# The entry of a SwiGLU FFN in a hybrid decoder layer: weights prepared in three steps, two products taken early, matmul operands moved by 32 bytes

## The chip, the cores and the metric

The kernel runs on one core of one Trainium2 chip. The metric is the device time of one execution in microseconds (us); the time of a kernel is the median of its runs.

## What is computed

One decoder layer on x of 512 tokens by 1024 channels, float32: an RMSNorm and an input projection, an RWKV-7 group and a sparse-attention group side by side, an output projection that is added to x, and then the part that this change concerns, a dense SwiGLU with its own norm, added again, and a last norm:

```python
def swiglu(x, w_gate, w_up, w_down):
    return (jax.nn.silu(x @ w_gate) * (x @ w_up)) @ w_down
...
        h = h + jnp.concatenate([y_r, y_n], axis=-1) @ w_out[l]
        h = h + swiglu(rms_norm(h, norm_ffn[l]), w_gate[l], w_up[l], w_down[l])
    return rms_norm(h, norm_final)
```

The FFN is 2816 wide, so the gate and up products are 512 x 1024 x 5632 together.

## The kernel before, in words

**Precision.** A float32 product is made of three matmuls (`mm3`, L162 to L165): each operand is split into a rounded part `hi` (a copy on ACT, L144) and the rest `lo` (a subtraction on DVE, L146), and hi x hi, hi x lo and lo x hi are accumulated. So each operand costs one ACT and one DVE instruction (`split`, L140) before PE can use it, and each of its matmuls loads its own 128 x 128 weights.

**Gate and up.** Columns of w_gate and w_up are taken in 11 quarters of 256 columns (q = 0 to 10). A quarter multiplies a 2 x 2 block matrix (two halves of the tokens by two halves of the channels, A11, A12, A21, A22) with a 2 x 2 block of weights (gate and up by two halves of the channels, B11, B21, B12, B22) in seven products instead of eight. On the side of A these need sums S1 to S4 of the blocks, on the side of the weights T1 to T4. The order on PE is B11 x A11, B21 x A12, T2 x S2, T1 x S1, T3 x S3, B22 x S4, T4 x A22. A product (`prod`, L1168) is 24 matmuls of 256 columns; a quarter is 168, the FFN's 11 quarters 1848. The weights are the stationary operand, A the moving one. The products are collected by DVE and ACT (L1189 to L1212).

**Weights of a quarter** (`weight_side`, L1112): SP issues loads of 512 KB for B11, B21, the gate half of T1, B22 and the up half of T3; POOL issues two DMAs that add w_up onto T1 (L1141) and T3 (L1142); DVE forms T2 = T1 + B22 (L1145) and T4 = T2 + B21 (L1150); each of the seven is split. Splits go in turn to the two buffers of tag whi and the two of wlo; of quarter 0 B11 and B21 go to tag b8. The raw data lie in wraw, and T1 to T3 in t4 for even quarters and in one slot of L for odd ones.

**The norm ahead of it** (`ffn_norm`, L1070). The output projection (`accumulate`, L1011) finishes the token tiles t = 0 to 3 one after the other; after each, DVE adds the residual (L1163), ACT squares and sums (L176, L177), DVE scales (L1076, xn), PE transposes (L1086), ACT copies out of PSUM (L1088). Tiles 0 and 1 are split into A11 and A12 at once. Tiles 2 and 3 first form S3, S1, S2, S4 with tiles 0 and 1 on DVE (L1099 to L1104) and split five operands each. Quarter 0's weights are prepared in the projection, ahead of its last four blocks (`ahead`, L1156).

**What sets the order.** Each engine runs its instructions in the order that a scheduler gave them when the program was built, in which `tc.high_priority()` brings work forward and an edge of `tc.issue_after(x)` keeps a block's instructions on the engine of x behind x. DMAs are issued by SP and POOL in order too, and an issue waits until the slot that it fills is free.

**Where the tiles lie.** The tiles of all tags lie in one SBUF range in a fixed layout. In every partition the slots of L, t4, wraw, whi and wlo begin 160 bytes past a multiple of 256, those of b8 and gin 32 bytes, that of kB 64, ident 128. The parts that a matmul reads begin whole multiples of 256 bytes into their slot. S2 lies in gin, S1 in kB, S4 in b8, A11, A12, S3 and A22 in L.

**Other users of the split weights.** `parts` (L148) serves the projections. For 512-column products (L163 to L165 with 128x512) the weights are stationary and the normed x in L moves, or in the output and down projections the other way round. In the first token projection (L301), the two compressions (`job_cmp1`, L666) and the four late token jobs (`job_vt`, `job_ks`, two `job_qs`, L602 to L647) the split weights are the moving operand of 256-column matmuls: 96 + 64 + 384 of them.

Of the kernel before, what the change touches and what calls it, by code (L numbers as in the profile page):

```python
# [46 lines left out]
def hybrid_layer(ctx: ExitStack, tc: tile.TileContext, x, positions, norm_mix, w_in, mu_shift, w0, w2, a0, a2,  # L47
# [12 lines left out]

    SB_BUFS = {"L": 4, "b8": 6, "t4": 4, "t2": 3, "wraw": 3, "whi": 2, "wlo": 2}
# [104 lines left out]

    def rstd_of(src, cut=()):
# [9 lines left out]
        ACT.activation(ss[:, 1:2], ss[:, 0:1], AF.Sqrt, scale=1.0 / D, bias=bias)  # L177
# [119 lines left out]
    for t in range(NT):  # L297
        next(norm)
        if t == 0:
            w0p = parts(raw0)  # L300
# [706 lines left out]
    gain2 = st([128, D], "t4")  # L1007
    nc.sync.dma_start(gain2, bcast_row(norm_ffn))
# [41 lines left out]


# [9 lines left out]
    def operand(tag):  # L1061
        v = st([128, 2, HK, 256], tag, dtype=F32R)
# [7 lines left out]
    def ffn_norm(src):  # L1070
        xn2 = st([128, 2, D], "b8")
        for t in range(NT):
            s = src(t)
            r = rstd_of(s)
            xn = xn2[:, t % 2]
            DVE.scalar_tensor_tensor(xn, s, r, gain2, op0=OP.mult, op1=OP.mult)  # L1076
# [3 lines left out]
            def put(name, v):  # L1080
                split(v, A[name][0][:, :, c], A[name][1][:, :, c])

            for kh in range(2):
                p = ps("s")
                for i in range(HK):
                    PE.transpose(p[:, i * 128:(i + 1) * 128], xn[:, (kh * HK + i) * 128:(kh * HK + i + 1) * 128], ident)  # L1086
# [4 lines left out]
            if t >= 2:  # L1091
# [268 lines left out]
```

## Time and profile before

| | us |
|---|---|
| median of 3 runs | 758.5 |
| lowest and highest | 755.49, 758.87 |
| the profiled execution | 762.32 |
| its span, first to last instruction | 760.6 |
| granted TensorE clock, mean over the span | 0.981 |

In the profile, PE is TensorE's matmuls, PEld its weight loads, DVE is VectorE, ACT ScalarE, POOL GpSimd, SP the engine that issues most DMAs. A matmul's row has its start and duration; matmuls overlap, so the rate is read from start to start. Names stand as out<-in by tag: `ps_ra<-gin,whi` is a matmul into a PSUM bank of tag ra that moves gin over weights in whi. The tag names b8 and t4, t2 appear as b and t. L146 and the like are lines of the kernel before.

### The profile page before, as it was taken

The page shows a single profiled execution, that of the slowest core. Times are in us where ns is not written, and L with a number is a line of the kernel's source. Part 1 is how long each engine was busy: PE and PEld are TensorE (multiplying, and loading weights), DVE is VectorE, ACT ScalarE, POOL GpSimd, SP SyncE. Part 2 cuts the span into 40 slices and gives each one's busy share as a digit, 9 for nine tenths or more (in the row PEclk, how much of TensorE's full clock was granted, in tenths as well). Part 3 has the DMA queues.
Part 4 walks back from the last instruction along what each step waited for, and adds up shares of the span by engine and source line. Part 5 has one row for each costly group of instructions (what it writes and reads, how often), then busy time and mean ns, then how long its engine had stood idle before and what let it go on. Part 6 is the DMA issues. An engine that isn't in the chain of part 4 may idle for free.

```text
span 760.6 us, 14951 instructions
## 1 busy us (share of the span) xinstructions
PE 726.2 (95%) x6045; PEld 636.6 (84%) x6045; DVE 593.1 (78%) x1089; ACT 399.1 (52%) x666; POOL 164.6 (22%) x262
## 2 busy tenths in 40 slices
PE   6999999998879999999998699999999999999996
PEld 6967878898867888767787699999999999877885
DVE  5488688879868888786459496969688789999835
ACT  6398735324366866756437534535344454465424
POOL 3210053048435542454001101111102001010000
PEclk7999999999999999999998999999999999999999
DMA  7723533100061000230415747695967629443302
GB/s 249 198 85 110 166 111 110 57 2 2 3 222 30 2 2 2 58 112 1 139 56 139 165 130 177 155 229 145 225 161 194 143 81 272 172 110 111 139 0 110
DMA packets 73467, 87.02 MB, mean 114 GB/s; under 512 B 4996, under 2 KB 62934, under 8 KB 73398
## 3 DMA queue, kind: packets, MB, share of 16 engines
q1 hardware_dynamic: 60694, 72.43, 29.2%
q0 software_dynamic: 12704, 13.63, 11.6%
q8 instruction: 47, 0.77, 0.4%
q14 instruction: 22, 0.18, 0.1%
HBM read 83.96 MB, written 2.10 MB: 113 GB/s over the span
## 4 chain that ended last, share of the span: by engine, by line
PE 67%; DVE 22%; DMA 4%; issue 3%; ACT 3%; POOL 0%; SPq 0%; DVEq 0%; ACTq 0%
PE ps_ra L164 6%; PE ps_ra L165 6%; PE ps_ra L163 6%; PE ps_pj L165 6%; PE ps_pj L163 6%; PE ps_pj L164 6%; PE ps_o L1001 3%; PE ps_s L165 3%; PE ps_s L163 3%; PE ps_s L164 3%; DVE wlo L146 3%; DVE L L146 3%; PE ps_pj L993 3%; DMA L<-in_w_up_dram 2%; DVE whi L146 2%
## 5 line engine op out<-in xcount | busy, mean ns | idle before, releaser
L144 ACT ACTIVATE whi<-wraw 128x1024 fp32r<-128x1024 f32 (+1 forms) x63 | 62.5, 1030 | 36.0 <-issue 9.1
L146 DVE TENSOR_TENSOR wlo<-wraw,whi 128x1024 fp32r<-128x1024 f32 (+1 forms) x46 | 58.9, 1306 | 16.3 <-ACT whi L144 12.8
L165 PE MATMUL ps_ra<-L,wlo 128*128 128x512 f32 (+2 forms) x144 | 50.9, 355 | 0.0
L990 POOL TENSOR_SCALAR whi<-whi,m,gates 128x128 f32<-128x128 f32 (+3 forms) x64 | 42.5, 680 | 37.1 <-DVE m L988 28.8
L164 PE MATMUL ps_ra<-L,whi 128*128 128x512 f32 (+2 forms) x136 | 47.4, 348 | 1.1 <-DVE L L146 1.1
L163 PE MATMUL ps_ra<-L,whi 128*128 128x512 f32 (+2 forms) x136 | 47.0, 346 | 1.2 <-ACT L L144 1.2
L164 PE MATMUL ps_pj<-L,whi 128*128 128x512 f32 (+1 forms) x128 | 45.7, 357 | 0.0
L163 PE MATMUL ps_pj<-L,whi 128*128 128x512 f32 (+1 forms) x128 | 45.1, 357 | 0.0
L165 PE MATMUL ps_pj<-L,wlo 128*128 128x512 f32 (+1 forms) x120 | 41.2, 343 | 0.0
L987 ACT ACTIVATE whi<-whi,m 128x128 f32<-128x128 f32 (+3 forms) x64 | 35.4, 554 | 9.5 <-DVE m L986 8.3
L163 PE MATMUL ps_ra<-whi,L 128*128 128x256 f32 (+1 forms) x108 | 35.7, 332 | 0.2 <-ACT L L144 0.2
L164 PE MATMUL ps_ra<-wlo,L 128*128 128x256 f32 (+1 forms) x108 | 35.7, 330 | 0.2 <-DVE wlo L146 0.2
L165 PE MATMUL ps_ra<-whi,L 128*128 128x256 f32 (+1 forms) x108 | 35.1, 327 | 0.0
L986 DVE CUSTOM_DVE_ANT_0 whi<-ps_s,negb 128x128 f32<-128x128 f32 (+3 forms) x64 | 29.3, 484 | 5.9 <-PE ps_pj L993 2.5
L165 PE MATMUL ps_pj<-whi,L 128*128 128x256 f32 (+1 forms) x108 | 33.9, 315 | 0.0
L164 PE MATMUL ps_pj<-wlo,L 128*128 128x256 f32 (+1 forms) x108 | 33.8, 313 | 0.0
L163 PE MATMUL ps_pj<-whi,L 128*128 128x256 f32 (+1 forms) x108 | 33.6, 315 | 0.0
L1141 POOL DMA_DIRECT2D t<-in_w_up_dram x6 | 7.9, 1323 | 114.0 <-DVE whi L146 50.2
L165 PEld LDWEIGHTS ps_ra<-L,wlo 128*128 128x128 f32 (+1 forms) x144 | 27.2, 189 | 4.2 <-issue 0.5
L164 PEld LDWEIGHTS ps_ra<-L,whi 128*128 128x128 f32 (+1 forms) x136 | 25.6, 188 | 4.8 <-DVE L L146 1.3
L163 PEld LDWEIGHTS ps_ra<-L,whi 128*128 128x128 f32 (+1 forms) x136 | 25.7, 189 | 4.7 <-ACT L L144 1.4
L164 PEld LDWEIGHTS ps_pj<-L,whi 128*128 128x128 f32 x128 | 24.9, 195 | 3.4 <-DVE L L146 0.4
(685 smaller groups left out, 2561.2 us busy)
## 6 DMA issues: line engine op xcount, KB each, us to landing
wraw<-in_w_gate_dram SPq DMA_DIRECT2D x22, 512.0 KB
wraw<-in_w_in_dram SPq DMA_DIRECT2D x9, 1024.0 KB
wraw<-in_w_down_dram SPq DMA_DIRECT2D x9, 1024.0 KB
t<-in_w_up_dram POOLq DMA_DIRECT2D x12, 512.0 KB, 7.4
wraw<-in_w_up_dram SPq DMA_DIRECT2D x11, 512.0 KB
L<-in_w_up_dram POOLq DMA_DIRECT2D x10, 512.0 KB, 8.2
wraw<-in_w_out_dram SPq DMA_DIRECT2D x4, 1024.0 KB
wraw<-in_w_in_dram SPq DMA_DIRECT2D x6, 512.0 KB
```

The lines of the kernel that those rows point to most:

```text
L144: ACT.activation(hi, src, AF.Copy)
L146: (POOL if pool else DVE).tensor_sub(lo, src, hi.bitcast(F32))
L163: PE.matmul(o, lh, rh, start=start, stop=False)
L164: PE.matmul(o, lh, rl, start=False, stop=False)
L165: PE.matmul(o, ll, rh, start=False, stop=stop)
L986: DVE.tensor_tensor_reduce(pr[:, i], pS[:, i], negb[:, S - n:S], scale=-1.0, scalar=3e38, op0=OP.add, op1=OP.min, accum_out=m[:, i, 0:1])
L987: ACT.activation(pr[:, i], pr[:, i], AF.Exp, scale=-1.0, bias=m[:, i, 0:1], accum_out=m[:, i, 1:2])
L990: POOL.tensor_scalar(pr[:, i], pr[:, i], m[:, i, 2:3], gv[:, 1 + b0 + i, h:h + 1], op0=OP.mult, op1=OP.mult)
L993: PE.transpose(pT[:, j], prr[:, x, j * 128:j * 128 + 128], ident)
L1001: PE.matmul(po[q, 2 * g:2 * g + 2], vtok[:, j % (t + 1), b0 + j // (t + 1), g], pTs[:, par, j], start=False, stop=g == 1 and bs[-1] == 1 a ...
L1141: POOL.dma_start(t1, quarter(w_up, 0), accum_op=OP.add)
```

## The change

`weight_side` becomes a class `Weights` whose steps are called one by one: loads of B11 and B21 when it is made, `begin` (their splits), `load_rest` (the other loads and the adding DMAs), `middle` (T2, T1), `end` (T3, B22, T4). Quarter 0 does all but `end` ahead of the projection's last blocks, with B11, B21, T2 and T1 in b8. After the norm come, in program order, `begin` of quarter 1, kept behind the last tile's Sqrt and xn; `end` of quarter 0, kept behind the last split of S4; the first two products of quarter 0; the first two of quarter 1, kept on PE behind the last transpose; and the other five of quarter 0. From quarter 2 on the steps follow one another as before. The residual additions and the norm are given high priority, S1 and S3 change places in the norm, gain2 is loaded a little later. The slots of whi and wlo grow by 64 elements (256 bytes), paid for by a descriptor scratch of 2048 in place of 4096 bytes; the FFN's weights are placed 56 elements (224 bytes) into their slot, and split weights that move 8 elements (32 bytes), so that on L the moving operand begins 32 bytes behind the stationary one, modulo 256.

```diff
+    PAD = 64
-    def parts(raw, tags=("whi", "wlo"), pool=False, lo_pool=False):
+    def parts(raw, tags=("whi", "wlo"), pool=False, lo_pool=False, off=0):
         b, n = raw.shape[1:]
-        hi, lo = (st([128, 2048], tag, 2, F32R) for tag in tags)
-        v = [t[:, 0:b * n].rearrange("p (k n) -> p k n", n=n) for t in (hi, lo)]
+        hi, lo = (st([128, 2048 + PAD], tag, 2, F32R) for tag in tags)
+        v = [t[:, off:off + b * n].rearrange("p (k n) -> p k n", n=n) for t in (hi, lo)]
...
-            w0p = parts(raw0)
+            w0p = parts(raw0, off=8)
...
+    moving = [jobs[i][1] for i in (3, 5, 7, 9, 12, 13, 14, 15)]
...
-        wn = parts(raws.pop(0)) if raws else None
+        wn = parts(raws.pop(0), off=8 if jobs[n + 1][1] in moving else 0) if raws else None
...
-    def operand(tag):
-        v = st([128, 2, HK, 256], tag, dtype=F32R)
+    def operand(tag, off=0):
+        v = st([128, 2048 + (PAD if tag in ("whi", "wlo") else 0)], tag, dtype=F32R)[:, off:off + 2048]
+        v = v.rearrange("p (x k n) -> p x k n", x=2, n=256)
         return v[:, 0], v[:, 1]
...
-            r = rstd_of(s)
             xn = xn2[:, t % 2]
-            DVE.scalar_tensor_tensor(xn, s, r, gain2, op0=OP.mult, op1=OP.mult)
+            with tc.high_priority(offset=1000000 if t in () else None):
+                r = rstd_of(s)
+                last["xn"] = DVE.scalar_tensor_tensor(xn, s, r, gain2, op0=OP.mult, op1=OP.mult).ins
...
-                s3 = st([128, HK, 128], "t2")
-                DVE.tensor_sub(s3, a11, a21)
-                DVE.tensor_sub(a21, a22, a21)
-                DVE.scalar_tensor_tensor(a11, a21, -1.0, a11, op0=OP.mult, op1=OP.subtract)
+                s1 = st([128, HK, 128], "t2")
+                DVE.tensor_sub(s1, a22, a21)
+                DVE.tensor_sub(a21, a11, a21)
+                DVE.scalar_tensor_tensor(a11, s1, -1.0, a11, op0=OP.mult, op1=OP.subtract)
...
+        def put(self, name, v, tag=None):
+            if tag is None:
+                tag = ("whi", "wlo")[turn2[0] % 2]
+                turn2[0] += 1
+            o = operand(tag, 56 if tag != "b8" else 0)
+            split(v, *o)
+            setattr(self, name, o)
...
     def ahead():
-        first.append(weight_side(0, 2))
+        ws[0] = Weights(0)
+        ws[0].begin("b8")
+        ws[0].load_rest()
+        ws[0].middle("b8")
...
-        for f in range(2):
-            sl = slice(f * 512, f * 512 + 512)
-            DVE.tensor_add(x2[:, t, sl], banks[f], x2[:, t, sl])
-        next(norm)
+        with tc.high_priority():
+            for f in range(2):
+                sl = slice(f * 512, f * 512 + 512)
+                DVE.tensor_add(x2[:, t, sl], banks[f], x2[:, t, sl])
+            next(norm)
...
+    ws[1] = Weights(1)
+    with tc.issue_after(last["sq"]), tc.issue_after(last["xn"]):
+        ws[1].begin()
+    with tc.issue_after(last["S4"][0]), tc.issue_after(last["S4"][1]):
+        ws[0].end()
+    first_products(0)
+    with tc.issue_after(last["pe"]):
+        first_products(1)
+    last_products(0)
+    for q in range(1, NF // 2):
+        if q > 1:
+            ws[q] = Weights(q)
+            ws[q].begin()
+        ws[q].load_rest()
+        ws[q].middle()
+        ws[q].end()
+        if q > 1:
+            first_products(q)
+        last_products(q)
...
-    nc = _bacc.Bacc("TRN2", target_bir_lowering=False, num_devices=1, dynamic_dma_scratch_size=4096)
+    nc = _bacc.Bacc("TRN2", target_bir_lowering=False, num_devices=1, dynamic_dma_scratch_size=2048)
```

`first_products(q)` and `last_products(q)` are the old loop's body cut behind the second product; the buffers u and g0 of quarter 1 lie in t4 and smask.

## Rows read from the trace of the kernel before

**Rows 1.** The page's parts 1 and 5: busy us, share, count; busy, mean ns, idle.
```profile
PE 726.2 (95%) x6045; PEld 636.6 (84%) x6045; DVE 593.1 (78%) x1089; ACT 399.1 (52%) x666; POOL 164.6 (22%) x262
...
L144 ACT ACTIVATE whi<-wraw 128x1024 fp32r<-128x1024 f32 (+1 forms) x63 | 62.5, 1030 | 36.0 <-issue 9.1
L146 DVE TENSOR_TENSOR wlo<-wraw,whi 128x1024 fp32r<-128x1024 f32 (+1 forms) x46 | 58.9, 1306 | 16.3 <-ACT whi L144 12.8
```

**Rows 2.** By stage: us; PE, PEld, DVE, ACT, POOL busy (count); PEclk, DMA share, GB/s.
```profile
380.00:404.50 24.50, 24.50 (x115) 20.33 (x114) 15.24 (x21) 12.36 (x20) 0.00 (x0) 1.00 0.13 43
404.50:441.60 37.10, 27.98 (x193) 26.64 (x192) 27.44 (x38) 19.89 (x31) 5.21 (x4) 0.86 0.69 156
...
481.60:642.50 160.90, 160.37 (x1346) 160.16 (x1345) 133.65 (x148) 73.82 (x83) 17.95 (x14) 1.00 0.69 176
...
143.00:204.00 61.00, 57.38 (x746) 54.61 (x745) 55.12 (x130) 19.93 (x36) 31.48 (x68) 0.97 0.01 2
```

**Rows 3.** The timeline of PE at the entry: start us, duration us, [idle before <-releaser].
```profile
404.33 0.27 PE L1086 MATMUL ps_s<-ident,b 128*128 128x128 f32 x1
407.37 0.47 PE L1086 MATMUL ps_s<-ident,b 128*128 128x128 f32 x1 [2.01 <-ACT L L1088]
411.12 0.58 PE L164 MATMUL ps_pj<-L,b 128*128 128x256 f32 x1 [1.36 <-DVE L L146]
420.36 0.38 PE L163 MATMUL ps_ra<-L,whi 128*128 128x256 f32 x1 [1.23 <-ACT L L144]
437.39 0.39 PE L165 MATMUL ps_pj<-L,whi 128*128 128x256 f32 x1 [3.26 <-DVE whi L146]
441.63 0.28 PE L164 MATMUL ps_ra<-L,wlo 128*128 128x256 f32 x1
```

**Rows 4.** The timeline of PE: first matmuls of products in the third quarter.
```profile
461.56 0.28 PE L163 MATMUL ps_s<-L,whi 128*128 128x256 f32 x1
464.44 0.28 PE L163 MATMUL ps_pj<-L,wlo 128*128 128x256 f32 x1
467.32 0.28 PE L163 MATMUL ps_ra<-gin,whi 128*128 128x256 f32 x1
470.17 0.28 PE L163 MATMUL ps_s<-kB,wlo 128*128 128x256 f32 x1
472.99 0.28 PE L163 MATMUL ps_pj<-L,whi 128*128 128x256 f32 x1
...
481.58 0.28 PE L163 MATMUL ps_pj<-L,wlo 128*128 128x256 f32 x1
```

**Rows 5.** The timeline of PE: eight transposes of the last tile, merged.
```profile
416.78 1.04 PE L1086 MATMUL ps_s<-ident,b 128*128 128x128 f32 x8
```

**Rows 6.** The timeline of DVE at the entry.
```profile
404.11 1.22 DVE L146 TENSOR_TENSOR wlo<-t,wlo 128x1024 fp32r<-128x1024 f32 x1
405.25 0.68 DVE L1163 TENSOR_TENSOR L<-ps_rb,L 128x512 f32<-128x512 f32 x1
...
413.46 1.27 DVE L1076 SCALAR_TENSOR_TENSOR b<-L,ss,t 128x1024 f32<-128x1024 f32 x1
...
424.23 0.69 DVE L146 TENSOR_TENSOR b<-L,b 128x512 fp32r<-128x512 f32 x1
...
434.98 1.23 DVE L1145 TENSOR_TENSOR L<-L,wraw 128x1024 f32<-128x1024 f32 x1 [5.79 <-DMA L<-in_w_up_dram]
```

**Rows 7.** The timelines of ACT, POOL and SP (SPq issues DMAs) around the entry.
```profile
409.87 1.05 ACT L176 ACTIVATE t<-L 128x1024 bf16<-128x1024 f32 x1
...
429.18 1.29 POOL L1141 DMA_DIRECT2D L<-in_w_up_dram  x1 [11.57 <-DVE t L1196]
430.34 1.43 POOL L1142 DMA_DIRECT2D L<-in_w_up_dram  x1
...
385.65 0.37 SPq L1125 DMA_DIRECT2D wraw<-in_w_gate_dram  x1
```

**Rows 8.** The timeline of DVE in the ninth quarter.
```profile
593.89 1.22 DVE L1145 TENSOR_TENSOR L<-L,wraw 128x1024 f32<-128x1024 f32 x1 [6.05 <-DMA L<-in_w_up_dram]
```

More of the change, by code (lines that the diff above doesn't have):

```diff
@@ L1080, in put @@
             def put(name, v):
-                split(v, A[name][0][:, :, c], A[name][1][:, :, c])
+                hi, lo = (o[:, :, c] for o in A[name])
+                last[t] = last[name] = ACT.activation(hi, v, AF.Copy).ins, DVE.tensor_sub(lo, v, hi.bitcast(F32)).ins
             for kh in range(2):
@@ L1154, in hybrid_layer, with __init__, quarter, begin @@
-    first = []
+    class Weights:
+        def __init__(self, q):
+            def quarter(w, kh):
+                return w[kh * 512:kh * 512 + 512, q * 256:q * 256 + 256].rearrange("(k p) n -> p k n", p=128)
+            r = st([128, 2, HK, 256], "wraw")
+            self.b11, self.b21 = r[:, 0], r[:, 1]
+            nc.sync.dma_start(self.b11, quarter(w_gate, 0))
+            nc.sync.dma_start(self.b21, quarter(w_gate, 1))
+            self.q, self.quarter = q, quarter
+        def put(self, name, v, tag=None):
[5 more added lines that the diff above has]
+            setattr(self, name, o)
+        def begin(self, tag=None):
+            with tc.high_priority():
+                self.put("B11", self.b11, tag)
+                self.put("B21", self.b21, tag)
+        def load_rest(self):
+            self.b22 = st([128, 2048], "wraw")[:, 0:1024].rearrange("p (k n) -> p k n", n=256)
+            if self.q % 2:
+                tt = st([128, 4, HK, 256], "L")
+                self.t1, self.t2, self.t3 = (tt[:, i] for i in range(3))
+            else:
+                self.t1, self.t2, self.t3 = (st([128, HK, 256], "t4") for _ in range(3))
+            nc.sync.dma_start(self.t1, self.quarter(w_gate, 0))
+            nc.sync.dma_start(self.b22, self.quarter(w_up, 1))
+            nc.sync.dma_start(self.t3, self.quarter(w_up, 0))
+            with tc.high_priority():
+                POOL.dma_start(self.t1, self.quarter(w_up, 0), accum_op=OP.add)
+                POOL.dma_start(self.t3, self.quarter(w_up, 1), accum_op=OP.add)
+        def middle(self, tag=None):
+            with tc.high_priority():
+                DVE.tensor_add(self.t2, self.t1, self.b22)
+                self.put("T2", self.t2, tag)
+                self.put("T1", self.t1, tag)
+        def end(self):
+            with tc.high_priority():
+                self.put("T3", self.t3)
+                self.put("B22", self.b22)
+                DVE.tensor_add(self.t2, self.t2, self.b21)
+                self.put("T4", self.t2)
@@ L1176, in prod, with first_products @@
         return o
-    hid, hid4 = [], []
-    for q in range(NF // 2):
+    hid, hid4, part = [], [], {}
+    def first_products(q):
         if q % 2 == 0:
-            h4 = st([128, 4, S], "b8") if q < NF // 2 - 1 else st([128, 2, S], "t4")
-            hid4.append(h4)
-        hq = h4[:, q % 2 * 2:q % 2 * 2 + 2]
-        hid += [hq[:, j] for j in range(2)]
-        w = weight_side(q) if q else first[0]
-        u, g0, v, u1 = (st([128, 2, 256], tag) for tag in ("t2", "t2", "t2", ("lora", "smask")[q % 2]))
-        p = prod(w["B11"], A["A11"])
+            part["h"] = st([128, 4, S], "b8") if q < NF // 2 - 1 else st([128, 2, S], "t4")
+            hid4.append(part["h"])
+        hq = part["h"][:, q % 2 * 2:q % 2 * 2 + 2]
+        hid.extend(hq[:, j] for j in range(2))
+        w = ws[q]
+        u, g0 = st([128, 2, 256], "t4" if q == 1 else "t2"), st([128, 2, 256], "smask" if q == 1 else "t2")
+        p = prod(w.B11, A["A11"])
         with tc.high_priority():
             ACT.activation(u, p, AF.Copy)
-        p = prod(w["B21"], A["A12"])
+        p = prod(w.B21, A["A12"])
         with tc.high_priority():
@@ L1258, in hybrid_layer @@
         a11, a21, a12, a22 = (h[:, :, x] for h in (one, two) for x in (left, right))
-        first, last = n == 0, n == 1
+        lead, end = n == 0, n == 1
         t1, t2 = block4(a, 0, "wraw"), block4(b, 1, ("gin", "kB")[n])
-        t3 = st([128, 4, 512], "wraw") if first else None
-        t3 = [t3[:, 2 * i:2 * i + 2] if first else st([128, 2, 512], "t4") for i in range(2)]
+        t3 = st([128, 4, 512], "wraw") if lead else None
+        t3 = [t3[:, 2 * i:2 * i + 2] if lead else st([128, 2, 512], "t4") for i in range(2)]
         for i in range(2):
@@ L1266, in hybrid_layer @@
         DVE.tensor_sub(a21, a22, a21)
-        multiply(m1, a_side(a11), b_side(t1), first, last)
+        multiply(m1, a_side(a11), b_side(t1), lead, end)
         DVE.tensor_add(a11, a21, a11)
```

72 lines of the change are left out of this document (22 added, 50 removed).

## Prediction

> **What bounds the kernel now.** I read the page's engine list first: PE is busy 726.2 us of 760.6, DVE 593.1 [rows 1]. That says matmuls bound most of the time, and leaves two questions: where PE waits, and how fast it goes where it doesn't. The table by stage answers the first: the entry of the FFN, 404.5 to 441.6 us, has PE busy for 27.98 of 37.1 us at a granted clock of 0.86, where the stretch before it has no gap and a clock of 1.00 [rows 2]. In the ten quarters behind it PE has no gap to speak of (160.37 of 160.9), while DVE has 133.65. So the FFN's quarters are bound by the spacing of matmuls, its entry by something else.
>
> The entry in PE's timeline: after the output projection's last matmul PE gets eight transposes at 404.33, waits 2.01 us for ACT, 1.36 for DVE, 1.23 for ACT at 420.36, and 3.26 for DVE at 437.39; the second quarter begins at 441.63 [rows 3]. In 404.33 to 441.63, 37.3 us, lie the first quarter's 168 matmuls at 0.119 us (20.0 us, a quarter's length: 461.56 to 481.58 [rows 4]) and 24 transposes: eight take 1.04 us, so with the last one's own 0.27 taken off (1.04 - 0.27)/7 = 0.11 each [rows 3, 5], 2.6 us. The rest, 37.3 - 20.0 - 2.6 = **14.7 us, is lost at the entry**, idle or at the low clock: 22 matmuls from 437.39 to 441.63 are 0.193 apart, behind the 3.26 us wait, so at the lower of the two clock levels. 14.7 is the most the entry can give back.
>
> Why it waits: DVE has hardly a gap from 404.11 to 424.9 [rows 6]. In front of the norm's work it runs four splits of late weights and the L1150 add, five at 1.22 us, so the last tile's normalised rows come at 413.46 though its residual was added at 405.25; its Square on ACT starts at 409.87 only [rows 6, 7]. The last A operand is written at 424.9. Then DVE's head is the L1145 add of the *second* quarter, which waits 5.79 us for an accumulating DMA issued at 429.18 [rows 6, 7]; the whi split that PE waits for stands behind it on DVE. That is PE's 3.26 us.
>
> The second question: 24 matmuls of 256 columns each make a product. Read from product start to product start, they take 2.88 us with A in L, 2.85 with gin, 2.82 with kB [rows 4]: 0.1200, 0.1188 and 0.1175 each. Weights and column counts are alike, only the moving operand's tile differs, and those begin 0, 128 and 160 bytes past the weights modulo 256. So the place of the operands bears on the spacing, or at least nothing in these rows says otherwise.
>
> **The change part by part.**
> *T1 and T2 of quarter 0 into b8.* whi and wlo are in use by the output projection until 404.5; b8 isn't, so these two splits (2.44 us of DVE) can run before 404, where DVE has gaps. *T3, B22, T4 behind the last S4*: two splits and the add leave the window (3.66). *The second quarter's B11 and B21* come in behind the last tile's xn (2.44). DVE's work in the window goes down by 6.1 - 2.44 = 3.7 us. *Norm at high priority*: Square follows 405.25 + 0.68 directly, so xn of the last tile starts some 4 us earlier; ACT's and DVE's own work is the same. The order S1, S3 in place of S3, S1 exchanges equal operations: 0. So the last A operand should come at about 420 rather than 424.9.
>
> *Early products.* The first two products of quarter 0 need tiles 0 and 1 alone; quarter 1's too. That is 4 x 2.88 = 11.5 us of PE work to lie beside the norm of tiles 2 and 3, where it had 5.8 (in part at the low clock). PE then has: from 404.5 5.8 us, transposes, 5.8 us, to about 417; S2 of the last tile, five DVE operations ahead of the last, comes at about 417. Queued behind first_products(1) on PE is all the rest of quarter 0; its gate loads were issued at 385.65 and found room [rows 7]; I take it that they still come in time, since no row shows the new order.
>
> *A wait goes; what is late next?* Quarter 1's T2 needs the L slot that the last A operand frees. From there to the T2 split's end before: free at 424.9, accumulate issued at 429.18, add from 434.98 [rows 6, 7], then 1.22 for the add and 1.03 + 1.31 for a split on ACT and DVE (their mean durations [rows 1]), 13.6 us. Quarter 0's five remaining products cover 14.3 us, less the 3 us by which they start before the slot is free: a new wait of about 2 us. The order of SP's and POOL's queues past this is unchanged in kind.
>
> Entry: 14.7 lost, less 2 for this new wait, less 1.7 for what remains idle before S2: **-11 us**. Ends: -14.7 (all of it) and -4 (only the five DVE operations leave, the rest of the chain is as late as before).
>
> *Addresses.* PAD is 256 bytes and the scratch shrinks by 2048, both multiples of 256, so the tags stay where they are, and off=56 (224 bytes) puts the weights 32 bytes below L. Of the FFN's 1848 matmuls, 1008 with A in L (4 products in ten quarters, 2 in the first) go from 0 to 32 apart; 504 with gin or b8 go from 128 to 160, the offset of the 0.1175 row; 240 with kB from 160 to 192. For 32 apart no row exists. Nearest rows: 0.1175 (160 apart) above, and below the eight transposes of 1.04 us, 0.110 a step as above [rows 5], whose operands are 96 apart. I take the middle, 0.1137, since neither is nearer: 1008 x (0.1200 - 0.1137) = **-6.4 us**, with ends -10 (0.110), -2.5 (0.1175) and +2.5, the same step the wrong way, since nothing excludes a loss. gin and b8: 504 x 0.0013 = -0.7. kB: 0, within 0.6. Outside the FFN: 160 matmuls of the compression and of the first projection at -0.006, half of it on the path: -0.5. The 384 of the four late token jobs gain nothing: there, 143 to 204 us, DVE is busy 55.12 of 61 us [rows 2] and sets the pace; without that cover they'd give 2.4. The 512-column products stay 0 apart.
>
> The rows show a spacing that differs with the tile. The Trainium skill (TensorE: Matmul & The Clock Gate, Part 2, step 1) says that weights and moving operand are read over two independent ports, so loading the next weights takes nothing from the running matmul. By that the offset would be worth 0 and the sum -11; the rows agree in that the effect is small, but not that it is nothing.
>
> *gain2's load moved, and the smaller scratch*: gain2 is issued a few instructions later in program order, still ahead of the first norm: 0. The scratch holds descriptors of accumulating DMAs, which the rows show two at a time at the most [rows 7]: 0. Both are bounded by one landing of 512 KB, 5.7 us (429.18 to the add at 434.98), once, if they came late or waited, and by nothing on the side of a gain, since neither removes work.
>
> Faster quarters lean harder on DVE's waits: one like L1145's 5.79 recurs at 593.89 with 6.05 [rows 8], where the ten quarters' whole PE idle time is 0.53 [rows 2]. I add +1. **Sum: -11 - 6.4 - 0.7 - 0.5 + 1 = -17.6.** The profiled execution took 762.32 us; 762.3 - 17.6 = 744.7. It lies 3.8 above the median of the runs, 758.5, so the forecast for a median is 741.
>
> **Rivals.**
> *Addresses pay nothing (chance 0.19).* The 0.1200 against 0.1175 belongs to the tile or to what DVE and ACT write meanwhile; quarters stay at 20.0 us. For it: no row at 32. Against: the rows repeat alike through the quarter. Time: 758.5 - 11 + 1 = 748.5. The page's rule above leads here.
> *The entry's wait only moves (0.13).* T2 of quarter 1, or S2, ends last as late as now: the DMA's 13.6 us chain is barely covered. Then -4 there and -7.6 from addresses: 747.
> *The change doesn't do what it says (0.10).* The scheduler orders DVE as before, and 32 apart is like 0: 757, within the noise.
> *Slower (0.07).* DVE is served in order, and middle's add for the next quarter, at high priority, waits for an accumulating DMA with evacuations and splits behind it. At the entry such a wait cost PE 3.26 idle and, at the low clock, 22 x 0.074 = 1.6 us more, some 5 us. With quarters of 19 us in place of 20 less is left to cover it. Ten quarters are behind the entry; four at 5 us cancel the gain, five give 758.5 - 17.6 + 25 = 766. Against it: the one repeat cost 0.53 at most [rows 2, 8].
>
> **How the numbers follow.** A change under 0.5% (3.8 us) can't be told from none here. The forecast, both parts paying within their ends, has 0.51; with the two rivals that still gain over 3.8 us, 0.19 and 0.13, faster has 0.83. Same has 0.10, slower 0.07. Low end: entry -14.7, addresses -11, 732; a little is left below that. High end: entry -4 with nothing from addresses, 754.5, so 755. The forecast's own range is 733 to 750.
>
> **What would show it.** Right: quarters of 18.9 to 19.3 us with products on L under 2.8 us; the fifth product's start within 13 us of the output projection's end; no PE gap over 2 us between; the last A operand near 420; clock near 1.0 in the entry. Wrong: products of 2.88 us still (first rival); a gap before T2 of quarter 1 of over 4 us (second); DVE waits of 6 us before L1145's successor with PE gaps in several quarters (slower).

## The result, and the profile after

| | before | changed |
|---|---|---|
| median of 14 runs each, on one chip | 758.65 | 753.22 |
| lowest and highest | 755.49, 763.34 | 750.21, 757.06 |
| ratio, 95% interval | | 0.9928, 0.9911 to 0.9944 |
| span of the profiled execution | 760.6 | 751.5 |
| granted TensorE clock, mean | 0.981 | 0.979 |

The change makes the kernel 5.4 us faster (0.72%), where 17.6 were forecast. The direction held and the size did not: less than a third came. 753.2 lies within the outer ends of the forecast (732 and 755) and outside its own range of 733 to 750.

The page's engine list and its groups for the split, after (they answer to [rows 1]):

```profile
PE 720.7 (96%) x6045; PEld 630.3 (84%) x6045; DVE 592.5 (79%) x1089; ACT 399.6 (53%) x666; POOL 165.1 (22%) x262
...
L145 ACT ACTIVATE whi<-wraw 128x1024 fp32r<-128x1024 f32 (+1 forms) x63 | 62.7, 1032 | 40.7 <-issue 11.7
L147 DVE TENSOR_TENSOR wlo<-wraw,whi 128x1024 fp32r<-128x1024 f32 (+1 forms) x46 | 58.4, 1295 | 15.6 <-ACT whi L145 12.1
```

The same counts at the same durations; PE is busy for 5.5 us less. By stage, with the columns of [rows 2]:

```profile
403.50:440.00 36.50, 29.81 (x241) 28.35 (x240) 28.68 (x41) 20.93 (x34) 3.74 (x3) 0.95 0.51 130
440.00:447.00 7.00, 6.54 (x31) 6.24 (x32) 5.62 (x7) 4.11 (x5) 1.47 (x2) 0.53 0.72 150
447.00:475.00 28.00, 28.00 (x241) 28.00 (x240) 24.64 (x29) 11.63 (x14) 3.29 (x3) 1.00 0.89 226
475.00:635.00 160.00, 160.00 (x1370) 159.82 (x1370) 136.93 (x151) 76.11 (x85) 19.83 (x16) 1.00 0.73 183
```

The entry still holds 6.7 us in which PE is idle, and after it comes a stretch of 7 us at a mean granted clock of 0.53, most of it at the lower of the two levels. PE's timeline at the entry, against [rows 3] (start, duration, idle before and its releaser):

```profile
405.58 0.38 PE L164 MATMUL ps_pj<-L,b 128*128 128x256 f32 x1
...
419.13 0.28 PE L164 MATMUL ps_s<-kB,b 128*128 128x256 f32 x1
...
439.79 0.58 PE L164 MATMUL ps_ra<-kB,whi 128*128 128x256 f32 x1 [5.98 <-ACT whi L145]
...
441.05 0.58 PE L166 MATMUL ps_ra<-kB,whi 128*128 128x256 f32 x1 [0.46 <-DVE whi L147]
```

The early products do what they were for: from 405.58 to 433.8 PE runs almost without a gap through both quarters' first products and quarter 0's other five. The four small waits of before (2.01, 1.36 and 1.23 in [rows 3], and one of 1.13) are gone. Then one wait of 5.98 us takes their place, for quarter 1's T1 and T2. The timelines of DVE, of SP's DMA issues and of POOL's, in this order, show where it comes from:

```profile
422.38 0.69 DVE L1090 TENSOR_TENSOR b<-L,b 128x512 fp32r<-128x512 f32 x1
...
438.60 1.22 DVE L1163 TENSOR_TENSOR L<-L,wraw 128x1024 f32<-128x1024 f32 x1 [5.91 <-DMA L<-in_w_up_dram]
```

```profile
423.10 0.37 SPq L1154 DMA_DIRECT2D L<-in_w_gate_dram  x1
423.51 0.51 SPq L1156 DMA_DIRECT2D L<-in_w_up_dram  x1
424.24 0.37 SPq L1155 DMA_DIRECT2D wraw<-in_w_up_dram  x1
425.37 0.37 SPq L1156 DMA_DIRECT2D t<-in_w_up_dram  x1
426.50 0.37 SPq L1130 DMA_DIRECT2D wraw<-in_w_gate_dram  x1
426.92 0.61 SPq L1131 DMA_DIRECT2D wraw<-in_w_gate_dram  x1
```

```profile
427.46 1.30 POOL L1158 DMA_DIRECT2D L<-in_w_up_dram  x1 [9.85 <-DVE t L1228]
438.89 1.29 POOL L1159 DMA_DIRECT2D L<-in_w_up_dram  x1 [10.13 <-issue]
```

The last A operand is written at 423.07. It frees the slot of L; the gate load is issued at once, the accumulating DMA at 427.46, and it lands at 438.58 (DVE's add starts there): 11.1 us, where it took 5.7 before [rows 6, 7]. Six loads of 512 KB, its own gate half among them, were issued ahead of it in 4 us.

The quarters, against [rows 4] (first matmuls of the products of the fourth quarter):

```profile
477.27 0.28 PE L164 MATMUL ps_pj<-L,wlo 128*128 128x256 f32 x1
480.07 0.28 PE L164 MATMUL ps_ra<-L,whi 128*128 128x256 f32 x1
482.87 0.28 PE L164 MATMUL ps_s<-gin,wlo 128*128 128x256 f32 x1
485.73 0.28 PE L164 MATMUL ps_pj<-kB,whi 128*128 128x256 f32 x1
488.45 0.28 PE L164 MATMUL ps_ra<-L,wlo 128*128 128x256 f32 x1
...
496.88 0.28 PE L164 MATMUL ps_ra<-L,whi 128*128 128x256 f32 x1
```

In this quarter a product on L takes 2.80 us (2.88 before), on gin 2.86 (2.85), on kB 2.72 (2.82), and the whole 19.61 (20.02). In the seven quarters behind it gin takes 2.82 and a quarter 19.57.

**A ledger.** All traces are read by the same three marks in PE's timeline: the end of the output projection's last matmul, the first matmul of the fourth quarter, the end of the FFN's last matmul. us; ratios are to runs of before on the same chip. The second trace of a kernel shows how far one trace can be trusted: the stages behind the projection repeat within 1 us, those that can stall within 2.4. The first column, ahead of most of the change, runs from 401.8 to 406.9, so the kernels are compared by the columns behind it and by the ratios, and not by their spans.

| kernel | start to projection's end | to 4th quarter | to the FFN's end | rest | span | ratio, 95% |
|---|---|---|---|---|---|---|
| before | 404.5 | 77.1 | 161.1 | 117.9 | 760.6 | |
| before, 2nd trace (e11) | 402.8 | 77.8 | 160.3 | 117.6 | 758.5 | |
| changed | 403.4 | 73.8 | 156.8 | 117.5 | 751.5 | 0.9928 (0.9911 to 0.9944) |
| changed, 2nd trace (a2) | 402.7 | 73.8 | 158.7 | 119.9 | 755.0 | 0.9933 (0.9908 to 0.9957) |
| e1 entry alone | 404.1 | 73.0 | 160.3 | 116.2 | 753.6 | 0.992 (0.9899 to 0.9942) |
| e2 addresses alone | 405.3 | 75.8 | 157.5 | 119.1 | 757.6 | 0.9954 (0.9936 to 0.9971) |
| e3 T in b8 | 405.1 | 92.2 | 159.4 | 118.6 | 775.2 | 1.0165 (1.0139 to 1.019) |
| e4 quarter 2's loads held | 404.7 | 70.6 | 158.7 | 118.6 | 752.7 | 0.9902 (0.9878 to 0.9926) |
| e5 offset 192 | 405.4 | 73.4 | 158.7 | 118.9 | 756.4 | 0.9934 (0.9909 to 0.9959) |
| e7 entry alone, scratch 4096 | 403.0 | 72.6 | 160.3 | 116.6 | 752.4 | 0.9934 (0.9913 to 0.9955) |
| e8 T in b8, first | 401.8 | 71.6 | 158.1 | 118.9 | 750.5 | 0.9903 (0.9887 to 0.9918) |
| e9 changed, scratch 4096 | 406.8 | 73.7 | 158.7 | 118.6 | 757.7 | 0.9944 (0.9924 to 0.9965) |
| e12 early T, scratch 4096 | 406.4 | 65.5 | 156.7 | 118.7 | 747.4 | 0.9845 (0.9817 to 0.9873) |
| e13 the same, offset 192 | 406.8 | 65.9 | 157.1 | 119.1 | 748.9 | 0.9854 (0.9825 to 0.9884) |
| e14 early T, no offsets | 405.5 | 66.1 | 160.3 | 116.2 | 748.2 | 0.9885 (0.9853 to 0.9917) |
| e15 join's add on POOL | 406.9 | 64.9 | 156.8 | 128.9 | 757.5 | 0.9995 (0.9972 to 1.0019) |

### The profile page after: what moved, and what is told of

The parts are those of the page before. It is cut to its first block, busy times and chain, and to the rows that moved or that the text cites. A ratio compares the mean times of both kernels' runs of the same rounds, so it can differ in the third digit from the quotient of the medians.

```text
span 751.5 us, 14937 instructions
## 1 busy us (share of the span) xinstructions
PE 720.7 (96%) x6045; PEld 630.3 (84%) x6045; DVE 592.5 (79%) x1089; ACT 399.6 (53%) x666; POOL 165.1 (22%) x262
## 4 chain that ended last, share of the span: by engine, by line
PE 66%; DVE 23%; DMA 5%; issue 3%; ACT 2%; POOL 0%; SPq 0%; DVEq 0%; ACTq 0%
PE ps_ra L166 6%; PE ps_ra L165 6%; PE ps_ra L164 6%; PE ps_pj L166 6%; PE ps_pj L164 5%; PE ps_pj L165 5%; PE ps_o L1006 3%; DVE wlo L147 3%; PE ps_s L166 3%; PE ps_s L164 3%; PE ps_s L165 3%; DMA L<-in_w_up_dram 3%; PE ps_pj L998 3%; DVE L L147 2%; DVE whi L147 2%
## 5 line engine op out<-in xcount | busy, mean ns | idle before, releaser
L166 PE MATMUL ps_ra<-L,wlo 128*128 128x512 f32 (+2 forms) x136 | 48.0, 354 | 0.0
L165 PE MATMUL ps_ra<-L,whi 128*128 128x512 f32 (+2 forms) x128 | 44.1, 345 | 0.0
L166 PE MATMUL ps_pj<-L,wlo 128*128 128x512 f32 (+1 forms) x128 | 43.9, 343 | 0.1
L164 PE MATMUL ps_ra<-L,whi 128*128 128x512 f32 (+2 forms) x128 | 43.8, 344 | 0.0
L164 PE MATMUL ps_ra<-whi,L 128*128 128x256 f32 (+1 forms) x108 | 34.4, 321 | 0.5 <-ACT L L145 0.5
L166 PE MATMUL ps_ra<-whi,L 128*128 128x256 f32 (+1 forms) x108 | 34.0, 316 | 0.0
L166 PEld LDWEIGHTS ps_ra<-L,wlo 128*128 128x128 f32 (+1 forms) x136 | 25.1, 185 | 4.0 <-issue 0.5
L166 PEld LDWEIGHTS ps_pj<-L,wlo 128*128 128x128 f32 x128 | 24.5, 191 | 3.7 <-DVE wlo L147 0.9
L164 PEld LDWEIGHTS ps_pj<-L,whi 128*128 128x128 f32 x128 | 24.4, 190 | 3.8 <-ACT whi L145 0.8
L165 PEld LDWEIGHTS ps_pj<-L,whi 128*128 128x128 f32 x128 | 24.4, 190 | 3.5 <-DVE L L147 0.4
```

What stands on the lines that cost most here:

```text
L164: PE.matmul(o, lh, rh, start=start, stop=False)
L165: PE.matmul(o, lh, rl, start=False, stop=False)
L166: PE.matmul(o, ll, rh, start=False, stop=stop)
```

## The experiments

**The two parts one by one.** e1 takes the offsets out of the changed kernel:

```diff
-            o = operand(tag, 56 if tag != "b8" else 0)
+            o = operand(tag)
...
-            w0p = parts(raw0, off=8)
+            w0p = parts(raw0)
...
-        wn = parts(raws.pop(0), off=8 if jobs[n + 1][1] in moving else 0) if raws else None
+        wn = parts(raws.pop(0), off=0) if raws else None
```

> The changed kernel with all operand offsets at 0, so the spacing of before (L 0 apart, gin and b8 128, kB 160) with the new order of the entry. Theory A (read from the two traces: the entry gives little because quarter 1's T2 comes 6 us late behind its accumulating DMA, and the addresses give 4.8 us: 1008 x 0.0033 on L, 240 x 0.0030 on kB, 504 x 0.0006 on gin and b8, 0.5 outside): quarters of 20.0 us again, the 6 us gap of PE before quarter 1's T2 stays, time 758.0, that is 0.6 below before. Theory B (the addresses give nothing in time): 753.2, as the changed kernel. Theory C (the forecast's sizes for the addresses, 7.6, and the entry a loss): 760.8, slower than before.

e2 puts the offsets, the larger slots and the smaller scratch alone into the kernel before.

> The kernel before with the offsets alone (and the larger slots and smaller scratch they need), the entry in its old order. Theory A: quarters of 19.65 us, L products 2.80, the entry's gaps of before (2.01, 1.36, 1.23, 3.26) stay; time 758.6 - 4.8 = 753.8. Theory B: 758.6. Theory C: 751.0.

> The changed kernel once more, so that it stands beside the runs of this call on the same chip, and for a second trace. If the parts add up (0.992 for the entry alone, 0.9954 for the addresses alone), its ratio to before is 0.987 to 0.988; if its first ratio holds, 0.993, with 0.991 to 0.994 as the interval, the two parts give less together than one by one.

Measured: the entry alone 0.992, the addresses alone 0.9954, both 0.9933. In the stages theory A was right: quarters of 20.0 us in e1 and 19.6 in e2, the gap before quarter 1's T2 stays in e1 (5.61 us). In the total it was wrong: e1 was as fast as the changed kernel, not slower by 4.8. The two parts don't add up: together they would give 0.987 (0.989 with e7's 0.9934 for the entry alone, which the intervals hardly part from 0.993). The ledger says where it is lost: with offsets (e2, and both traces of the changed kernel) the quarters are 1.6 to 3.5 us shorter and the rest is 1.3 to 3.7 us longer than in e1.

**What quarter 1's T1 and T2 wait for.** e4 holds quarter 2's gate loads, the last 1 MB issued ahead of the accumulating DMA:

```diff
+            if q == 2:
+                with tc.issue_after(last["acc"]):
+                    for k in range(2):
+                        POOL.memset(r[:, k, 0, 0:1], 0.0)
```

(`last["acc"]` is the second accumulating DMA of the quarter before.)

> The changed kernel with the two loads of quarter 2's gate weights (1 MB, issued at 426.50 and 426.92, right before quarter 1's accumulating DMA at 427.46) held until the second accumulate of quarter 1 has been issued; two one-element writes by POOL hold them. Theory F (the accumulate's 11.1 us, against 5.7 before, are the queue of transfers issued ahead of it): it lands within 8 us, by 435.5, the gap of PE shrinks from 6.0 to 3 us or less, and the time falls by 3 to 4, to 749.5. Rival G (the 11.1 us have another cause, such as the smaller scratch of descriptors): it lands at 438.5 as now, 753.2. Quarter 2 starts late, and the time rises, if its loads are needed sooner than 447.

The accumulating DMA of e4 on POOL, and PE behind it:

```profile
428.89 1.30 POOL L1162 DMA_DIRECT2D L<-in_w_up_dram  x1 [9.68 <-DVE t L1232]
436.80 1.29 POOL L1163 DMA_DIRECT2D L<-in_w_up_dram  x1 [6.60 <-issue]
```

```profile
437.70 0.39 PE L164 MATMUL ps_ra<-kB,whi 128*128 128x256 f32 x1 [2.62 <-ACT whi L145]
```

It lands at 436.49 (the next issue follows 0.3 us later), 7.6 us after its issue, and the gap falls from 5.98 to 2.62: transfers ahead of it made up 3.5 of the 11.1 us (theory F). The entry is 3.2 us shorter; in the time this can't be told from the changed kernel, the intervals overlap.

e7 is e1 with no padding and the scratch of before (`PAD = 0`, `dynamic_dma_scratch_size=4096`).

> The entry alone (offsets 0) with the slots and the descriptor scratch of before (4096 in place of 2048 bytes). If the smaller scratch serves one accumulating DMA at a time (in the changed kernel each is issued 0.3 us after the one before has landed; before they were issued 1.2 us apart), pairs are issued together again: quarter 1's second accumulate goes from 439.3 to 430, its first lands no sooner (about 439, the same queue of transfers ahead of it), the gap of PE before T2 stays at 5.6 to 6, and the time is that of the entry alone within 0.3% (0.992). If the scratch also makes the first one late, the gap falls below 3 us and the ratio to 0.988.

```profile
427.27 1.30 POOL L1158 DMA_DIRECT2D L<-in_w_up_dram  x1 [9.91 <-DVE t L1228]
428.49 1.40 POOL L1159 DMA_DIRECT2D L<-in_w_up_dram  x1
```

That is e7's timeline of POOL. With 4096 bytes the second one is issued 1.2 us behind the first, with 2048 only when the first has landed (438.89 above). The first still lands at 437.59, the gap is 5.32, the time that of e1. So the smaller scratch does put accumulating DMAs in a row, but it did not cause this gap.

e3 moves quarter 1's T1, T2, T3 and B22 out of the late slot of L, into b8:

```diff
+            if self.q == 1:
+                ta, tb = (st([128, 2, HK, 256], "b8") for _ in range(2))
+                self.t1, self.t2, self.t3, self.b22 = ta[:, 0], ta[:, 1], tb[:, 0], tb[:, 1]
-            if self.q % 2:
+            elif self.q % 2:
```

> The changed kernel with quarter 1's T1, T2, T3 and B22 data in two slots of b8, which come free at 412 to 413 us, in place of one slot of L, which comes free at 423, and one of wraw, free at 424. Theory A (the slot's release starts the chain load, accumulate, add, split that PE waits for): the accumulating DMA is issued by 418 and lands by 425, no PE gap over 1 us between 413 and 455, clock 1.0 there, and the 6.0 + 0.5 us idle and the 2.6 us lost at the low clock go: 753.2 - 9 = 744. Rival D (the next thing is as late: DVE's splits, or T3's accumulate served after T1's): a gap of 3 us or more stays, 748 to 751. Rival E (the gap is not on the path of the end): 753.

Every theory missed: 1.6% slower, with a PE gap of 24.83 us. The slots were free, but the order on the queues had changed. The timelines of SP's issues and of POOL in e3:

```profile
429.19 1.35 SPq L1158 DMA_DIRECT2D b<-in_w_gate_dram  x1
```

```profile
429.51 1.30 POOL L1162 DMA_DIRECT2D L<-in_w_up_dram  x1 [9.99 <-DMA L<-in_w_gate_dram]
...
453.26 1.28 POOL L1162 DMA_DIRECT2D b<-in_w_up_dram  x1 [4.71 <-issue]
```

The scheduler put quarter 1's DMAs behind quarter 3's, which now could have the L slot, and POOL serves them one after the other. e8 writes them ahead in the program:

```diff
+    with tc.high_priority():
+        ws[1].load_rest()
     last_products(0)
     for q in range(1, NF // 2):
...
-        ws[q].load_rest()
-        ws[q].middle()
+        if q > 1:
+            ws[q].load_rest()
+            ws[q].middle()
+        else:
+            with tc.issue_after(last["S4"][0]), tc.issue_after(last["S4"][1]):
+                ws[q].middle()
```

> As the run with quarter 1's T data in b8, where SP and POOL served them behind quarter 2's and 3's and PE waited 24.83 us, but with their loads and accumulates written ahead of quarter 2's, so that they come first on both queues, and T2's add kept behind S4 on DVE. Theory A (PE's gap before quarter 1's T2 is the late start of load and accumulate): the loads are issued by 414.5, the accumulate by 419 and landed by 425, no PE gap over 1 us between 413 and 455, granted clock 1.0 from 420 to 460, the output projection's end to quarter 3's start 65.5 us, where the changed kernel has 73.82; the time falls by 8 us, ratio to before 0.982. Rival D (T3's accumulate or a slot of whi or wlo is late next): a gap of 3 us or more stays, ratio 0.988. Rival E (the gap is not on the path of the end): 0.993.

The accumulate is issued at 412.81 and lands at 420.75; the gap before T1 and T2 is gone (nothing over 0.42 us up to 441). Theory A holds for that wait, rival D for what followed: from 441.60 PE waits 3.93 us for a split that stands on DVE behind this add of *quarter 2* (e8's timeline of DVE):

```profile
441.92 1.23 DVE L1167 TENSOR_TENSOR t<-t,wraw 128x1024 f32<-128x1024 f32 x1 [7.90 <-DMA t<-in_w_up_dram]
```

Its accumulating DMA was issued at 431.63, 0.3 us after the one before had landed: now the scratch matters. e12 is e8 with 4096 bytes (two temporaries of the compression go from a tag of their own into t2 to make room), e9 the changed kernel with the same.

> Quarter 1's T data in b8 and first on the queues, with the scratch of 4096. In the run with 2048 the accumulates stood in a row (412.81, 421.07, 431.63, 442.21, each 0.3 us after the landing of the one before) and PE waited 3.93 us at 441 for a split behind DVE's wait for quarter 2's accumulate. Theory J: they are issued in pairs, quarter 2's lands by 436, no PE gap over 1.5 us between 413 and 470, output projection's end to quarter 3 in 66.5 (71.63 there), ratio to before 0.981. Rival K (the queue of transfers, not the scratch, makes them late): the gap of 3 to 4 us stays, ratio 0.990 as with 2048.

> The changed kernel with the descriptor scratch of before (4096 bytes; two small temporaries of the compression moved into t2 make the room). Theory J (with the faster quarters the accumulating DMAs, served one at a time, come late, so DVE waits and gives back at the join with the down projection what the addresses bring): pairs of accumulates overlap again, DVE's waits for accumulates between 460 and 650 us fall from 16.9 to under 9, no PE gap over 0.6 in the quarters and none before the first product of the down projection (1.31 in the changed kernel's second trace); quarter 3 to the FFN's end 156.5 to 157 in place of 158.70, the rest 117 in place of 119.88; ratio to before 0.988. Rival K (the scratch is worth nothing): 0.993, as the changed kernel, with the same gaps.

e12, the timeline of POOL and the entry's row of the table by stage:

```profile
416.75 1.32 POOL L1162 DMA_DIRECT2D b<-in_w_up_dram  x1 [55.55 <-PE ps_s L1095]
420.95 1.30 POOL L1163 DMA_DIRECT2D b<-in_w_up_dram  x1 [2.89 <-DVE L L1090]
423.26 1.29 POOL L1162 DMA_DIRECT2D t<-in_w_up_dram  x1 [1.00 <-DVE L L1110]
```

```profile
406.40:446.00 39.60, 38.46 (x314) 36.93 (x312) 34.30 (x46) 25.28 (x38) 7.78 (x6) 1.00 0.91 219
```

Three are in flight at once, quarter 2's has landed at 430.87, no gap exceeds 0.70 us, the granted clock is 1.00 through the entry, and the entry takes 65.5 us, 12 less than before. The kernel stands at 0.9845 (0.981 was expected), faster than both before and the changed kernel (0.9933 on this chip; the intervals are apart). e9 gains nothing by the scratch alone (0.9944): there the L slot is what comes late.

**Does the spacing follow the addresses?** e5 sets `operand(tag, 16 ...)` and gives the 512-column weights `off=16`, the moving ones `off=48`.

> The changed kernel with other offsets: moving operand 192 bytes past the stationary one modulo 256 for A in L (32 in the changed kernel), 64 for gin and b8 (160), 96 for kB (192), and 192 for the split projections with 512 columns and stationary weights (0), while output and down projections stay 0 apart. Theory H (the spacing follows the difference of the addresses modulo 256, whatever the tile): L goes from 0.1167 to 0.114 to 0.115, the value of kB at 192, kB leaves it; four products of a quarter 2.74 in place of 2.80 us, the time falls by 1008 x 0.0025 = 2.5 us plus or minus 1.5 for gin, b8 and kB. Rival I (the spacing belongs to the tile): L stays at 0.1167, kB at 0.1145. For 512 columns: 0.2266 at 0 apart; by H with the same 0.0055 step, 0.221 at 192.

```profile
478.82 0.28 PE L164 MATMUL ps_pj<-L,wlo 128*128 128x256 f32 x1
481.54 0.28 PE L164 MATMUL ps_ra<-L,whi 128*128 128x256 f32 x1
484.26 0.28 PE L164 MATMUL ps_s<-gin,wlo 128*128 128x256 f32 x1
487.09 0.28 PE L164 MATMUL ps_pj<-kB,whi 128*128 128x256 f32 x1
489.97 0.28 PE L164 MATMUL ps_ra<-L,wlo 128*128 128x256 f32 x1
```

The fence shows e5's timeline of PE, first matmuls of the fourth quarter's products. Theory H: L, moved to 192, now has the 2.72 us that kB had at 192 in the changed kernel; kB, moved to 96, has 2.88; gin at 64 has 2.83. So the spacing goes with the difference: L and kB take the same 2.72 at 192, and kB, gin and b8 the same 2.82 at 160. It is not all of it: within one trace the same product can take two values (a2: kB 2.72 or 2.83, gin 2.82 to 2.88), where in both traces of before each product that doesn't stall keeps its own. With 512 columns it goes the other way: eight matmuls from the first line below in e5 (192 apart) and in the changed kernel (0 apart):

```profile
109.83 0.39 PE L164 MATMUL ps_ra<-L,whi 128*128 128x512 f32 x1
...
111.46 0.40 PE L165 MATMUL ps_ra<-L,whi 128*128 128x512 f32 x1
```

```profile
109.66 0.39 PE L164 MATMUL ps_ra<-L,whi 128*128 128x512 f32 x1
...
111.25 0.39 PE L165 MATMUL ps_ra<-L,whi 128*128 128x512 f32 x1
```

1.63 against 1.59 us for seven steps. 288 such matmuls at +0.006 are 1.7 us lost, and the quarters, 19.43 us where nothing stalls, stall three times (158.7 in the ledger); e5 as a whole gains nothing (0.9934). e13 moves the FFN's weights alone, in e12:

> The same with the FFN's weights placed so that L lies 192 bytes past them (gin and b8 64, kB 96), the 512-column products left 0 apart. From the rows of the runs at these differences (L 0.1152 against 0.1169, gin and b8 0.1178 against 0.1184, kB 0.1195 against 0.1145): -1.7 - 0.3 + 1.2 = -0.8 us against the run beside it, if PE is what bounds the quarters; no difference if DVE's waits bind. At most 0.3% either way.

As expected: 0.9854 against 0.9845, quarters of 19.4 that stall once (20.6).

> The kernel before once more, for a second trace to set beside the ledgers of this chip: if the stages are stable from run to run, output projection's end to quarter 3 at 77.1, quarter 3 to the FFN's end 161.1, the rest 117.9, each within 1; time 760.8 as the median on this chip.

That held within 0.8 in each stage, and the time was 761.21. The span is 2 us shorter than the first trace's, so a difference of that size between two single traces says nothing.

**Where the addresses' gain goes.** e14 is e12 with e1's edit, the same instructions in the same order.

> The version with early T data and scratch 4096, with all offsets at 0; instruction order unchanged on every engine. Theory M (the addresses bring 0.4 us a quarter, and the join gives 2 us of it back because DVE's work there ends no earlier): output projection's end to quarter 3 in 66.7 (65.53 with offsets), quarter 3 to the FFN's end 160.3 (156.75), the rest 116.5 (118.72), so 2.5 us slower than the run with offsets, ratio to before 0.988 against 0.9845. Rival N (nothing is given back): rest as with offsets, 118.7, 4.7 slower, 0.991. Rival O (the addresses are worth nothing in the end): 0.9845.

Theory M within 0.6 us in the stages: 66.1, 160.3, 116.2. The ratio is 0.9885 against 0.9845, as forecast, but on another chip, and the intervals overlap: the stages show it, the time alone does not. The offsets bring 3.6 us in the eight quarters and 0.6 in the entry, and the rest gives 2.5 back. Why: the DVE split that PE needs at the join, and PE's matmul on it, first e12, then e14:

```profile
646.03 1.24 DVE L147 TENSOR_TENSOR whi<-b,whi 128x1024 fp32r<-128x1024 f32 x1
```

```profile
647.33 0.73 PE L166 MATMUL ps_s<-L,whi 128*128 128x512 f32 x2 [0.98 <-DVE whi L147]
```

```profile
646.90 1.22 DVE L147 TENSOR_TENSOR whi<-b,whi 128x1024 fp32r<-128x1024 f32 x1
```

```profile
649.51 0.61 PE L166 MATMUL ps_s<-L,whi 128*128 128x512 f32 x2
```

DVE has no gap from 609 to beyond 675 us in either. Counted from the projection's end, the FFN's last matmul starts at 222.0 in e12 and 226.2 in e14, 4.2 apart; the split starts at 239.7 and 241.4, 1.7 apart. PE comes earlier by 4.2, DVE only by 1.7, and the join waits for DVE: 1.25 of the 2.5 us are lost at this row, most of the others at four rows up to 675 us. All traces bear it out. Take the distance from the start of the FFN's last matmul to the start of this split: it is 15.2 to 15.5 us in e1, e7 and e14, 16.4 to 16.9 in both traces of before and the first of the changed kernel, and 17.5 to 18.9 in the others with offsets (but for e15, below). The rest is 101.0 us more than this distance, within 0.05, in every trace but e15's. So the rest follows how far DVE lags behind PE at the join. e15 takes an addition of 2.31 us off DVE ahead of that split:

```diff
-        DVE.tensor_add(t2s[n], t2s[n], b21)
+        (DVE if n else POOL).tensor_add(t2s[n], t2s[n], b21)
```

> The version with early T data, scratch 4096 and offsets, with the first addition of L1353 (gin<-gin,wraw, 2.31 us) done by POOL in place of DVE. It stands on DVE ahead of the split that PE waits for (0.98 to 1.31 us at about 646 to 655). Theory M (DVE's backlog sets the join): that gap goes, the split comes 2.3 us earlier, the rest falls from 118.72 to 117.0 to 117.5, ratio to before 0.9825. Rival P (something else, such as the landing of the down weights, sets it): gap and rest unchanged, 0.9845; POOL's own addition could be late for the product that needs it, then slower.

```profile
638.32 27.77 POOL L1363 TENSOR_TENSOR gin<-gin,wraw 128x2048 f32<-128x2048 f32 x1 [14.22 <-DMA wraw<-in_w_down_dram]
666.04 2.45 POOL L1335 DMA_DIRECT2D t<-in_w_down_dram  x2
```

```profile
672.90 1.22 PE L164 MATMUL ps_s<-L,whi 128*128 128x512 f32 x2 [11.14 <-ACT L L145]
```

The fences are e15's timelines of POOL and PE. The wait of 0.98 us does go (the split starts at 643.57, 15.2 us behind the FFN's last matmul), so DVE's backlog set it. But POOL needs 27.77 us for what DVE does in 2.31, the accumulating DMAs behind it on POOL come late, and PE waits 11.14 us: 0.9995. The edit tells the cause of the small wait and is no remedy, and what the lighter DVE would have been worth in time stays unmeasured.

## Why the prediction was right or wrong

**The step that failed first: "a new wait of about 2 us."** It named the right place, the second rival's, and even the right chain: slot, gate load, accumulate, add, split. Its price was wrong. Start: the last A operand came at 423.07, not at about 420. Counted from the projection's end it came 19.6 us behind, against 20.4 before, so the norm's high priority gained 0.8 us where some 5 were forecast. "Square follows 405.25 + 0.68 directly" did not happen: the residual was done at 404.60, but ACT ran copies and splits until the Square, in the timeline of ACT after the change:

```profile
407.59 1.04 ACT L179 ACTIVATE t<-L 128x1024 bf16<-128x1024 f32 x1
```

Length: from the free slot to PE's matmul it took 16.7 us (423.07 to 439.79), not 13.6, since the accumulate took 11.1 us and not 5.7: five other loads had gone out ahead of it within 3.4 us, where before one did; e4 shows 3.5 us of this, e12 shows that an early start takes the wait away. 5.7 was also among the shortest such landings in the trace of before; part 6 of its page has the median, 8.2 us:

```profile
L<-in_w_up_dram POOLq DMA_DIRECT2D x10, 512.0 KB, 8.2
```

PE's work ahead of the wait lasted to 433.8, 2.5 us longer than the forecast's 417 + 14.3, which covered part of it. And the low clock behind the wait was not counted: the 27 matmuls from 439.79 on, at 0.21 or slower in place of 0.117, cost 3 us. With the 5.98 and 0.46 that is 9.4 us in place of 2. In the ledger the entry alone gave 4 to 5 us (from 77.1 and 77.8 to 73.0 and 72.6) in place of 11, so the second rival's -4 came near. That the rest of the step was sized right in sum shows in e12 and e14: without this wait the entry takes 65.5 to 66.1 us, 11 to 12 less than before, where the forecast was 11 by the entry and 1.9 by three quarters' addresses. The prediction asked "what is late next?" and then priced it by a row in which the queue was nearly empty.

**The second: the middle, 0.1137, for 32 apart.** Measured 0.1167 (2.80/24), where the four products on L of a quarter took 0.1197 on average before (2.88, 2.88, 2.86, 2.87). 1008 x 0.0030 is 3.0 us, not 6.4. The upper bound came from matmuls of the same kind, the lower from transposes of 128 columns in place of 256, 96 apart; at 96 apart the 256-column matmuls of e5 take 0.1200, so that row said nothing of them, and "neither is nearer" was wrong. kB was costed at 0 and gave 240 x 0.0042 = 1.0; gin and b8 gave 0.6 (2.85 to 2.82), as costed. Sum 4.6, or 0.45 a quarter (20.02 to 19.57).

**The third: the join was not looked at.** The sum let a quarter's gain pass to the end, with +1 for DVE's waits. The rest is 118.6 to 119.9 us with offsets (117.5 in the changed kernel's first trace alone) and 116.2 to 116.6 without, at the new entry. DVE's 133.65 of 160.9 us in the quarters [rows 2] did not tell it; a window on the join in the trace of before does. It has, like [rows 2], us, then PE, PEld, DVE, ACT, POOL, and DVE is busy for all 50 us:

```profile
642.00:692.00 50.00, 48.93 (x213) 39.00 (x213) 50.00 (x47) 30.36 (x33) 2.40 (x2) 1.00 0.54 149
```

**Addresses pay nothing** was false as a statement on matmuls (e2, e5, e14); in time, the changed kernel can't be told from the entry alone (0.9928 and 0.9933 against 0.992 and 0.9934), for the reason just given. The rule of the Trainium skill behind it (TensorE: Matmul & The Clock Gate, Part 2, step 1: weights and moving operand over two independent ports) does not cover what e5 shows: the spacing on L differs by 0.0067 us (0.1200 at 0, 0.1133 at 192) with the difference of the addresses alone.

**Right:** matmul spacing follows the place of the operands; the early products fill the norm's time; the waits that recurred in the quarters cost 2 us at the most in the changed kernel's two traces (156.8 and 158.7); the smaller scratch cost nothing in the changed kernel (e7, e9), and gain2's load nothing either (issued at 213 us, first used at 396). The reason given for the scratch was wrong all the same: two at a time were the most in the rows of before, but 2048 bytes let through one at a time, which cost e8 most of what parts it from e12. The 22 matmuls read as "at the lower of the two clock levels" were so in part (some 15 at 0.21, the others mostly at 0.12); the 1.6 us taken for them is right.

**The checks it named:** quarters of 18.9 to 19.3 (19.6), products on L under 2.8 (2.80), the fifth product within 13 us of the projection's end (419.13 - 403.45 = 15.7; the path to 417 had left 0.9 us for transposes, and the 22 there take some 2.4 at 0.11 each), no PE gap over 2 us (5.98), last A operand near 420 (423.07), clock near 1.0 (0.95, then 0.53): each failed, and the gap of over 4 us before quarter 1's T2 was the sign it had named for the second rival.

**Open:** the entry alone shortens the rest by 1.0 to 1.7 us against before (116.2 and 116.6 against 117.9 and 117.6) because DVE's split at the join stands 15.2 to 15.5 us behind the FFN's last matmul in place of 16.6 to 16.9; why DVE lags less there was not tried. In the quarters that stall by up to a microsecond (20.66 in a2, 20.62 in e13, 20.81 in before itself) PE waits for a wlo split that stands on DVE behind an add that waited 5.9 to 6.3 us for its accumulating DMA; why that lands in time in one trace and not in another is open. So is why 192 helps 256-column matmuls and hurts 512-column ones.

## What to carry to other kernels

Price a wait on a DMA by the queue that will stand ahead of it after the change, not by the row of before: slots that come free earlier send out loads that the late one then queues behind; move the critical load's issue, its buffer and its place on every in-order queue together. Against before, e3 moved the buffer alone and lost 12 us, e8 moved all three and won 7, e12 had room for several accumulating DMAs in flight besides and won 12. A shorter inner loop is worth only what the next stage's slower engine lets through, so lay a window on the join before counting it. Take a bound for an unseen operation from rows of its own kind.

## What the runs showed of the hardware

The spacing of 128x256 fp32r matmuls goes with (moving minus stationary address) modulo 256: 0.1192 to 0.1200 us at 0, 0.1167 at 32, 0.1179 at 64, 0.1200 at 96, 0.1188 at 128, 0.1175 at 160, 0.1133 at 192 (224 was not tried). At 160 and 192 single products of some traces take up to 0.1200 and 0.1179. With 512 columns 192 is the worse place: 0.233 against 0.227 at 0. With a scratch of 2048 bytes one accumulating DMA of 512 KB was in flight at a time, with 4096 up to three. An addition of 128x2048 took POOL 27.77 us beside a DVE that was busy for most of it, twelve times DVE's 2.31, while DVE's own splits stayed at 1.21 us; no run has the addition on POOL beside an idle DVE; the Trainium skill (GPSIMD Engine Reference, ahead of its section 1) has the Vector engine about twice as fast for such arithmetic, and here the measurement differs.
